# The even mixer's 31-tap convolution: from VectorE to TensorE, in four phases of the tokens and 32-column tiles

## The chip, the cores and the metric

One NeuronCore of one Trainium2 chip runs the whole program. The metric is the device time of one launch in microseconds (us). The engines are TensorE (PE; its weight loads are listed as PEld), VectorE (DVE), ScalarE (ACT), GpSimd (POOL) and SyncE (SP, which only issues DMAs). Each engine runs its own list of instructions in order, and that order is fixed when the program is built. TensorE has two clock levels, 1.2 and 2.4 GHz; the profile's granted clock is the share of the higher one.

## What is computed

A two-layer network for 512 tokens of width 1024 (even mixer, odd mixer), followed by a second two-layer block (a state-space mixer, an attention mixer, and an MLP and a gated embedding in each layer). Only the even mixer is touched:

```python
p = h @ w_in                                  # (512, 5120)
a_val, a_glu, a_gate, b_val, b_gate = split(p)
u = a_val * sigmoid(a_glu)
u = causal_depthwise_conv(u, conv_w, conv_b)  # 31 taps along the tokens, each channel by itself
u = silu(layernorm(u, ln_g, ln_b))            # over the 1024 channels
ya = u * silu(a_gate)
d = multiscale_pool_diff(b_val)               # windows of 2, 4, 8, 16 tokens
yb = (d @ pool_w + pool_b) * pool_scale * silu(b_gate)
return concat(ya, yb) @ w_out
```

All of it is float32.

## The kernel before

Activations lie transposed: a tile is 128 channels (partitions) by 512 tokens. Every large product is made of three TensorE passes (`mm3`, L284 to L286): weight and activation are each split into a high and a low part, and hi·hi, hi·lo and lo·hi are added. An output tile of 128 columns with 1024 inputs takes 24 such matmuls of 512 columns. Its weights (512 KB) come by one DMA from SP into `raw` (two buffers, L264); ACT makes `hi` (three buffers), and `lo = raw - hi` is made by POOL for the first 107 weight tiles and by VectorE after that (`prep`, `on_pool`). The even mixer's own weight tiles are numbers 0 to 57.

In `even` the order is as follows. Four eager output tiles run on the input before the norm; then `xg` (normed input, 8 tiles) is ready. For each of 8 channel tiles `c`, one output tile gives the value and one the gate, and VectorE makes `u` of them. All 31 taps of the convolution are VectorE instructions (`stt`, L240, one tap of one channel tile each) that add into a PSUM bank `cv`; two channel tiles run side by side. This block stands under `later(4000)`, which tells the planner that sets the order to let other work go first. Its last instruction for each channel tile also feeds `csum`, the sum over channel tiles. Then come the pooling branch (`pooled`, four groups), the mean (`mu`, a matmul of `csum` with ones, L554), the subtraction, squares and their sum, eight output tiles for `yb`, eight for the gate `a_gate` (inside which `rms_col` and `spread` of the norm lie, L337 and L366), and last the products `normed`, `gated`, `halved` and eight output tiles for `ya`.

Beside it runs `tables`, which prepares the state-space mixer of a later stage: eight rounds, each with small float32 matmuls (L963, L965, in 32-column tiles), transposes (L971, L989), many small POOL and VectorE operations, and some twenty DMAs from SP. Its matmuls have a very high priority on TensorE, its other work the lowest.

The planner works from its own estimate of times; if an operand comes later on the chip than it thought, the engine's queue waits there.

Of the kernel before, what the change touches and what calls it, by code (L numbers as in the profile page):

```python
# [7 lines left out]
F32 = mybir.dt.float32  # L8
# [3 lines left out]
AF = mybir.ActivationFunctionType  # L12
# [56 lines left out]


def host_layout(i):
    f = {}
# [25 lines left out]
    v.add("g_even", gcols(i["norm_even"][0]))  # L98
    v.add("conv_a_w", np.ascontiguousarray(i["conv_a_w"][0].reshape(KC, 8, 128).transpose(2, 1, 0)).reshape(128, 8 * KC))
    v.add("conv_a_b", cols(i["conv_a_b"][0]))  # L100
    v.add("ln_g", cols(i["ln_a_g"][0]))
# [33 lines left out]
    c.add("chunk", np.repeat(np.arange(64, dtype=np.float32)[None], 128, axis=0))  # L135
    c.add("half", np.repeat(np.repeat(np.eye(2, dtype=np.float32)[::-1], 64, axis=0), 16, axis=1))
    c.add("not0", np.repeat((np.arange(64) > 0).astype(np.float32)[None], 128, axis=0))
    f["consts"] = c.array()
# [18 lines left out]
class Kern:  # L157
# [5 lines left out]
    YA, LNP, SQB, TS = 3, 2, 3, (8, 0, 0)  # L163
    SQX, EPOS = (0, 2, 5), (0, 4)
    BOOST = 400
    on_pool = frozenset(range(107))

# [209 lines left out]
    def consts(self):  # L377
# [6 lines left out]
        self.ident, self.fix, self.eye16, self.chunk, self.not0 = (C(n) for n in ("ident", "fix", "eye16", "chunk", "not0"))  # L384
        self.half = C("half")
        self.halfpi = self.p_const.tile([128, 1], F32, name="halfpi")
# [26 lines left out]
    def even(self, h, behind_norm, extra, tables):  # L413
        nc = self.nc
        hw = self.L("hw", 1, F32, (128, 8 * KC))
        self.ts(hw, self.V("conv_a_w", 0, 8 * KC), 0.5, ALU.mult)

# [50 lines left out]

        us = []
        for c in range(8):  # L470
            th = self.L("th", 2)
            u = self.L("b", 9)
            if c < self.EAGER:
                pv, pg = first[2 * c:2 * c + 2]
                self.mul(th, pg, rs)
                pg = th
                self.mul(u, pv, rs)
                pv = u
            else:
                pv = self.mtile(xg)  # L480
                pg = self.mtile(xg)
            self.act(th, pg, AF.Tanh, scale=0.5)
            self.stt(u, th, 1.0, pv, ALU.add, ALU.mult)
            us.append(u)
            if c == self.EAGER - 1:
                if self.BN == 2:
                    behind_norm()
                extra()
        csum = None
        with self.later(4000):  # L490
            for c in range(0, 8, 2):
                cs = (c, c + 1)
                ps = [self.bank("cv") for _ in cs]
                for j in range(KC - 2, -1, -1):
                    s = KC - 1 - j
                    for q, y in zip(cs, ps):
                        w = hw[:, q * KC + j:q * KC + j + 1]
                        if s == 1:
                            self.act(y[:, 1:], us[q][:, :T - 1], AF.Identity, scale=w, bias=self.V("conv_a_b", q))
                            self.act(y[:, 0:1], self.ones[:, 0:1], AF.Copy, scale=self.V("conv_a_b", q))  # L500
                        else:
                            self.stt(y[:, s:], us[q][:, :T - s], w, y[:, s:], ALU.mult, ALU.add)
                for q, y in zip(cs, ps):
                    self.stt(us[q], us[q], hw[:, q * KC + KC - 1:q * KC + KC], y, ALU.mult, ALU.add)
                    if q == 1:
                        csum = self.L("b", 9)
                        self.add(csum, us[0], us[1])
                    elif q > 1:
                        self.add(csum, csum, us[q])
        conv = us  # L510

# [3 lines left out]
        def pooled(g):  # L515
            w = 2 << g
            ds[g] = []
            for c in range(2):
                pb = self.mtile(xg)
                v = self.L("v", 2)  # L520
                self.act(v, pb, AF.Copy)
                cur, sh = v, 1
                while sh < w:
                    n = self.L("pl", 3)
                    nc.scalar.copy(out=n[:, :sh], in_=cur[:, :sh])
                    self.add(n[:, sh:], cur[:, sh:], cur[:, :T - sh])
                    cur, sh = n, sh * 2
                o = w - 2
                self.mul(cur[:, :w], cur[:, :w], self.fix[:, o:o + w])
                self.stt(v, cur, 1.0 / w, v, ALU.mult, ALU.subtract)  # L530
                ds[g].append(self.split(v, self.LR("d", 6)))

        pooled(0)
        for g in range(4):
# [10 lines left out]
            for c in range(2):  # L545
# [5 lines left out]
                yb.append(self.split(t, self.LR("big", 16), self.V("pool_scale", 2 * g + c)))  # L551

        mu = self.bank("st")
        nc.tensor.matmul(mu, self.ones, csum, start=True, stop=True)  # L554
# [33 lines left out]
        def normed(c):  # L588
            self.mul(conv[c], conv[c], lrs)
            self.act(conv[c], conv[c], AF.Silu, scale=self.V("ln_g", c), bias=self.V("ln_b", c))  # L590

        def gated(c):
            self.mul(conv[c], conv[c], ga[c])

        def halved(c):
            ya.append(self.split(conv[c], self.LR("big", 16)))

# [1142 lines left out]
```

## Time and profile before

| | |
|---|---|
| time, median of 3 runs | 1914.96 us (1912.16 to 1916.82) |
| the profiled execution's own time | 1916.26 us |
| its span, first to last instruction | 1914.5 us |
| mean granted TensorE clock | 0.963 |
| TensorE busy | 1775.2 us (93%) |
| VectorE busy | 1258.0 us (66%) |
| POOL busy | 576.6 us (30%), of it 366 us in the first 500 us |
| DMA | 200.57 MB, mean 105 GB/s |

The even mixer's matmuls on `xg` start at 54 us and its last ones end near 442 us; the odd mixer follows at once. In the page, times are us, the mean of one instruction is in ns, and "idle before" is what the engine stood still ahead of a group, with the one that ended it behind the arrow. A TensorE matmul's duration contains its way through the array; the distance between starts is what it costs in a stream.

### The profile page before, as it was taken

The page shows a single profiled execution, that of the slowest core. Times are in us where ns is not written, and L with a number is a line of the kernel's source. Part 1 is how long each engine was busy: PE and PEld are TensorE (multiplying, and loading weights), DVE is VectorE, ACT ScalarE, POOL GpSimd, SP SyncE. Part 2 cuts the span into 40 slices and gives each one's busy share as a digit, 9 for nine tenths or more (in the row PEclk, how much of TensorE's full clock was granted, in tenths as well). Part 3 has the DMA queues.
Part 4 walks back from the last instruction along what each step waited for, and adds up shares of the span by engine and source line. Part 5 has one row for each costly group of instructions (what it writes and reads, how often), then busy time and mean ns, then how long its engine had stood idle before and what let it go on. Part 6 is the DMA issues. An engine that isn't in the chain of part 4 may idle for free.

```text
span 1914.5 us, 23189 instructions
## 1 busy us (share of the span) xinstructions
PE 1775.2 (93%) x8530; PEld 1426.4 (75%) x8530; DVE 1258.0 (66%) x1916; ACT 764.1 (40%) x1298; POOL 576.6 (30%) x606
## 2 busy tenths in 40 slices
PE   6998889799987797799999999999999999999997
PEld 5776667567766576687888888887778888888886
DVE  8999999976878768745432344478776642244456
ACT  3334332443654553224332242334665432233233
POOL 4889877683667643200000000023000000000002
PEclk7999989899998998899999999999999999999998
DMA  4233233333222378623222223333111222322322
GB/s 150 82 114 98 92 104 116 110 97 100 68 71 78 112 237 280 206 79 104 99 93 94 99 93 95 99 104 110 49 47 52 99 97 90 99 98 90 99 88 94
DMA packets 104290, 200.57 MB, mean 105 GB/s; under 512 B 26737, under 2 KB 57073, under 8 KB 104177
## 3 DMA queue, kind: packets, MB, share of 16 engines
q1 hardware_dynamic: 96496, 182.41, 29.6%
q0 software_dynamic: 2640, 8.65, 1.4%
q10 hardware_dynamic: 5040, 8.04, 1.2%
q8 instruction: 67, 1.10, 0.2%
q14 instruction: 47, 0.38, 0.1%
HBM read 176.38 MB, written 22.02 MB: 104 GB/s over the span
## 4 chain that ended last, share of the span: by engine, by line
PE 62%; DVE 24%; issue 4%; ACT 4%; POOL 3%; DMA 2%; SPq 0%; ACTq 0%; DVEq 0%; POOLq 0%
PE mm L284 18%; PE mm L285 17%; PE mm L286 17%; DVE cv L240 6%; DVE xs L228 2%; POOL lo L228 1%; DVE pl L228 1%; PE pv L1512 1%; DVE e L726 1%; DVE srr L228 1%; DVE xc L240 1%; ACT hi L225 1%; PE sc L285 1%; PE sc L284 1%; PE sc L286 1%
## 5 line engine op out<-in xcount | busy, mean ns | idle before, releaser
L225 ACT ACTIVATE hi<-raw 128x1024 fp32r<-128x1024 f32 (+1 forms) x280 | 292.1, 1045 | 646.9 <-PE mm L285 543.1
L228 DVE TENSOR_TENSOR lo<-raw,hi 128x1024 fp32r<-128x1024 f32 (+1 forms) x185 | 226.8, 1226 | 417.2 <-ACT hi L225 413.7
L286 PE MATMUL mm<-xg,lo 128*128 128x512 f32 x924 | 365.3, 396 | 4.6 <-POOL lo L228 4.6
L284 PE MATMUL mm<-xg,hi 128*128 128x512 f32 x924 | 366.5, 398 | 1.9 <-ACT xs L225 1.4
L285 PE MATMUL mm<-xg,hi 128*128 128x512 f32 x924 | 364.9, 396 | 0.0
L1326 POOL DMA_DIRECT2D pj<-proj x16 | 8.8, 548 | 1036.6 <-DVE t L240 795.8
L228 POOL TENSOR_TENSOR lo<-raw,hi 128x1024 fp32r<-128x1024 f32 (+1 forms) x95 | 234.3, 2469 | 117.5 <-ACT hi L225 106.9
L284 PE MATMUL mm<-hid,hi 128*128 128x512 f32 (+1 forms) x648 | 254.4, 393 | 1.3 <-DVE t L228 1.3
L285 PE MATMUL mm<-hid,hi 128*128 128x512 f32 (+1 forms) x648 | 253.9, 392 | 0.0
L286 PE MATMUL mm<-hid,lo 128*128 128x512 f32 (+1 forms) x648 | 253.7, 392 | 0.0
L286 PEld LDWEIGHTS mm<-xg,lo 128*128 128x128 f32 x924 | 176.6, 191 | 42.7 <-POOL lo L228 5.3
L284 PEld LDWEIGHTS mm<-xg,hi 128*128 128x128 f32 x924 | 176.4, 191 | 41.2 <-ACT xs L225 1.9
L285 PEld LDWEIGHTS mm<-xg,hi 128*128 128x128 f32 x924 | 176.6, 191 | 38.7 <-issue 1.2
L240 DVE SCALAR_TENSOR_TENSOR cv<-b,hw,cv 128x510 f32<-128x510 f32 (+28 forms) x232 | 158.7, 726 | 0.0
L284 PEld LDWEIGHTS mm<-hid,hi 128*128 128x128 f32 x648 | 121.7, 188 | 30.1 <-DVE t L228 1.5
L285 PEld LDWEIGHTS mm<-hid,hi 128*128 128x128 f32 x648 | 121.7, 188 | 28.6
L286 PEld LDWEIGHTS mm<-hid,lo 128*128 128x128 f32 x648 | 121.7, 188 | 28.5
L284 PE MATMUL mm<-y,hi 128*128 128x512 f32 x192 | 78.6, 409 | 5.4 <-ACT y L225 5.4
L286 PE MATMUL mm<-y,lo 128*128 128x512 f32 x192 | 76.7, 400 | 1.3 <-POOL lo L228 1.3
L285 PE MATMUL mm<-y,hi 128*128 128x512 f32 x192 | 76.8, 400 | 0.0
L285 PE MATMUL mm<-big,hi 128*128 128x512 f32 x160 | 68.2, 427 | 8.5 <-DVE big L240 7.6
L284 PE MATMUL mm<-big,hi 128*128 128x512 f32 x160 | 65.3, 427 | 8.5 <-DVE gt L240 5.8
(467 smaller groups left out, 3157.1 us busy)
## 6 DMA issues: line engine op xcount, KB each, us to landing
raw<-in_w_up SPq DMA_DIRECT2D x64, 512.0 KB
raw<-in_w_down SPq DMA_DIRECT2D x64, 512.0 KB
raw<-in_w_in_even SPq DMA_DIRECT2D x40, 512.0 KB
raw<-in_w_in_odd SPq DMA_DIRECT2D x24, 512.0 KB
raw<-in_w_out_even SPq DMA_DIRECT2D x16, 512.0 KB
raw<-in_w_glu SPq DMA_DIRECT2D x16, 512.0 KB
raw<-in_w_gate SPq DMA_DIRECT2D x16, 512.0 KB
raw<-in_w_out_odd SPq DMA_DIRECT2D x16, 384.0 KB
```

Of the source, the lines that this page charges most:

```text
L225: self.nc.scalar.activation(out=out, in_=in_, func=func, scale=scale, bias=bias)
L228: (eng or self.nc.vector).tensor_tensor(out=out, in0=a, in1=b, op=op)
L240: self.nc.vector.scalar_tensor_tensor(out=out, in0=a, scalar=s, in1=b, op0=op0, op1=op1)
L284: mm(out, hi[:, sl], xh, start=start, stop=False)
L285: mm(out, hi[:, sl], xl, start=False, stop=False)
L286: mm(out, lo[:, sl], xh, start=False, stop=stop)
L726: nc.vector.tensor_tensor_scan(out=y, data0=u[:, k], data1=x[:, k], initial=0.0, op0=ALU.mult, op1=ALU.add)
L1326: self.nc.gpsimd.dma_start(out=p, in_=pj[m])
L1512: mm(o, l, r[:, w], start=n == 0, stop=n == 6 * nk - 1)
```

## The change

The convolution leaves VectorE. For each channel tile the gated `u` is written with its tokens sorted into four phases (token mod 4), stored to DRAM (`cu`), and read back sixteen times by SP: for each quarter of 32 channels a tile `z` holds four groups of 8 channels side by side, and on its 128 partitions 8 channels times four phases times four shifts (0 to 3 places). A convolution of 31 taps then is, for each quarter and each group of 8 channels in it, three matmuls that add up (shifts of 0, 4 and 8 columns), in float32, with weights of 128 x 32 in which one column is one channel and one output phase: 48 matmuls a channel tile, each on one of four 32-column tiles of the array (`tile_position=(0, 32*g)`), of 128, 124 and 120 columns. The weights are spread over the block-diagonal form by VectorE (`taps`: three multiplications by a mask for each channel tile). ACT adds the bias and empties PSUM, and the result goes through DRAM again (`cy`, written from ACT's queue, read by SP) to come back as channels by tokens, still in phase order; `gated` puts the tokens back. The matmuls of channel tile c - 2 are traced behind the two output tiles of channel tile c. Apart from that the low parts of weight tiles 0, 2, ..., 56 move from POOL to VectorE.

```diff
-    on_pool = frozenset(range(107))
+    on_pool = frozenset(n for n in range(107) if n > 57 or n % 2)
...
+        def phases(c, u):
+
+            cu = self.dram.tile([128, T], F32, name=f"cu{c}")
+            nc.sync.dma_start(out=cu, in_=u)
+            zs = []
+            for q in range(4):
+                z = self.L("big", 16).rearrange("p (g t) -> p g t", g=4)
+                nc.gpsimd.memset(z[0:96, :, 0:3], 0.0)
+                for a in range(4):
+                    src = bass.AP(cu.tensor, cu.offset + 16384 * q, [[128, 32], [4096, 4], [1, 125 + a]])
+                    nc.sync.dma_start(out=z[32 * a:32 * a + 32, :, 3 - a:128], in_=src)
+                zs.append(z)
+            ready[c] = zs
+
+        def taps(c):
+            wd = self.L("wd", 2, F32, (128, 192))
+            nc.sync.dma_start(out=wd, in_=self.I["conv_a_w"][c])
+            self.act(wd, wd, AF.Copy, scale=0.5)
+            ws = []
+            for k in range(3):
+                w = self.L(*(("sq", self.SQB), ("gt", 3))[c % 2])
+                self.tt(w.rearrange("p (g d o) -> p g d o", g=16, d=8),
+                        wd[:, 64 * k:64 * k + 64].rearrange("p (g o) -> p g o", g=16).unsqueeze(2).to_broadcast([128, 16, 8, 4]),
+                        self.own.unsqueeze(1).unsqueeze(3).to_broadcast([128, 16, 8, 4]), ALU.mult, nc.gpsimd if c in self.TAPP else None)
+                ws.append(w)
+            ready[c] = ready[c], ws
+
+        def convolve(c):
+            zs, ws = ready.pop(c)
+            y = self.bank("cv")
+            for q in range(4):
+                for k in range(3):
+                    for g in range(4):
+                        w = ws[k][:, 32 * (4 * q + g):32 * (4 * q + g) + 32]
+                        with self.after():
+                            nc.tensor.matmul(y[32 * g:32 * g + 32, 128 * q + 4 * k:128 * q + 128], w, zs[q][:, g, 0:128 - 4 * k],
+                                             start=k == 0, stop=k == 2, tile_position=(0, 32 * g))
+            o = self.L("v", 2)
+            for q in range(4):
+                self.act(o[:, 128 * q:128 * q + 128], y[:, 128 * q:128 * q + 128], AF.Identity, bias=self.V("conv_a_b", 4 * c + q))
+            cy = self.dram.tile([T, 128], F32, name=f"cy{c}")
+            nc.scalar.dma_start(out=cy.rearrange("(q p) t -> p q t", p=128), in_=o.rearrange("p (q t) -> p q t", q=4))
+            conv[c] = self.L("b", 9)
+            nc.sync.dma_start(out=conv[c], in_=cy.rearrange("(h p) t -> h (p t)", p=4))
...
+            phases(c, u)
...
-        with self.later(4000):
-            for c in range(0, 8, 2):
...
-                            self.stt(y[:, s:], us[q][:, :T - s], w, y[:, s:], ALU.mult, ALU.add)
...
+            if c:
+                taps(c - 1)
+            if c > 1:
+                convolve(c - 2)
...
+                if g == 0:
+                    if c == 0:
+                        taps(7)
+                    convolve(6 + c)
...
+        csum = self.L("b", 9)
+        for c in range(1, 8):
+            self.add(csum, csum if c > 1 else conv[0], conv[c])
         mu = self.bank("st")
...
         def gated(c):
-            self.mul(conv[c], conv[c], ga[c])
+            v, ga[c] = ga[c], self.L("d", 6)
+            p4 = lambda x: x.rearrange("p (t o) -> p t o", o=4)
+            self.mul(p4(ga[c]), conv[c].rearrange("p (o t) -> p t o", o=4), p4(v))
```

## Rows read from the trace of the kernel before

**Rows 1.** The page: tenths of busy time in 40 slices of 47.9 us, two engines.
```profile
PE   6998889799987797799999999999999999999997
DVE  8999999976878768745432344478776642244456
```
**Rows 2.** Stretches of the even mixer: busy us (instructions) of each engine, clock, DMA.
```profile
54.00:180.00 126.00, 119.31 (x528) 94.01 (x527) 125.93 (x205) 47.38 (x99) 110.41 (x155) 0.97 0.32 102
180.00:250.00 70.00, 58.61 (x244) 45.20 (x243) 70.00 (x85) 25.51 (x60) 63.79 (x80) 0.93 0.34 105
250.00:310.00 60.00, 54.18 (x237) 41.52 (x236) 60.00 (x93) 21.26 (x45) 43.85 (x57) 0.94 0.35 103
...
340.00:390.00 50.00, 35.85 (x150) 26.22 (x150) 47.25 (x97) 25.70 (x61) 34.34 (x43) 0.85 0.40 115
390.00:442.00 52.00, 50.41 (x220) 38.53 (x221) 37.94 (x48) 21.31 (x35) 40.84 (x44) 0.95 0.31 93
```
**Rows 3.** TensorE's waits from 54 to 442 us: us, times, longest.
```profile
PE st L554 <- DVE b L228: 6.4, 1, 6.4
PE mm L284 <- DVE gt L240: 5.8, 1, 5.8
PE mm L286 <- POOL lo L228: 5.3, 3, 2.6
```
**Rows 4.** Groups on TensorE, 54 to 442 us: one of the large products.
```profile
L284 PE MATMUL mm<-xg,hi 128*128 128x512 f32 x288 | 117.3, 410 | 0.0
```
**Rows 5.** TensorE in order of time: start us, us, engine, line, operation.
```profile
434.57 0.40 PE L284 MATMUL mm<-big,hi 128*128 128x512 f32 x1
434.90 0.30 PE L965 MATMUL tab<-tq_wi,cbi 128*32 128x128 f32 x1
434.91 0.30 PE L963 MATMUL tab<-tq_wr,cbr 128*32 128x128 f32 x1
...
435.15 0.38 PE L965 MATMUL tab<-tq_wi,cbi 128*32 128x128 f32 x2
435.46 0.50 PE L285 MATMUL mm<-big,hi 128*128 128x512 f32 x1
435.80 0.40 PE L286 MATMUL mm<-big,lo 128*128 128x512 f32 x1
...
436.03 0.40 PE L284 MATMUL mm<-big,hi 128*128 128x512 f32 x1
```
**Rows 6.** The same view near 733 us: four 32-column tiles one after another.
```profile
732.44 0.68 PE L1100 MATMUL st<-ctile,xc 128*32 128x64 f32 x16 [4.81 <-DVE xc L228]
733.04 0.80 PE L284 MATMUL mm<-y,hi 128*128 128x512 f32 x1
733.64 0.63 PE L285 MATMUL mm<-y,hi 128*128 128x512 f32 x1
734.07 0.63 PE L286 MATMUL mm<-y,lo 128*128 128x512 f32 x1
```
**Rows 7.** Groups on VectorE, 54 to 442 us: the convolution, and a contended subtraction.
```profile
L240 DVE SCALAR_TENSOR_TENSOR cv<-b,hw,cv 128x510 f32<-128x510 f32 (+28 forms) x232 | 158.7, 726 | 0.0
L228 DVE TENSOR_TENSOR d<-v,d 128x512 fp32r<-128x512 f32 x8 | 14.0, 1754 | 0.0
```
**Rows 8.** Low parts of weights: POOL from 54 to 442 us.
```profile
L228 POOL TENSOR_TENSOR lo<-raw,hi 128x1024 fp32r<-128x1024 f32 x54 | 133.4, 2471 | 43.6 <-ACT hi L225 41.9 <-issue 1.6
```
**Rows 9.** Low parts of weights on VectorE, 500 to 1000 us.
```profile
L228 DVE TENSOR_TENSOR lo<-raw,hi 128x1024 fp32r<-128x1024 f32 (+1 forms) x42 | 50.5, 1205 | 91.1 <-ACT hi L225 90.9
```
**Rows 10.** ACT, 54 to 442 us: emptying a 128x128 piece of PSUM.
```profile
L225 ACT ACTIVATE tq_ks<-tab 128x128 f32<-128x128 f32 x8 | 2.1, 268 | 7.7 <-PE tab L965 7.7
```
**Rows 11.** SP's queue: issuing loads of 128 rows of 512 bytes.
```profile
676.39 2.46 SPq L1078 DMA_DIRECT2D gt<-tM  x4
```
**Rows 12.** A stretch in which SP issues such loads without a pause.
```profile
684.00:688.00 4.00, 4.00 (x19) 3.24 (x18) 1.17 (x1) 0.83 (x1) 1.85 (x1) 1.00 0.71 203
```
**Rows 13.** The chain of work, 240 to 395 us: a DMA from issue to landing.
```profile
290.05 2.83 DMA tO<-tq_wr
```
**Rows 14.** TensorE in order of time: the norm's matmuls, and the first on `ya`.
```profile
345.86 2.07 PE L554 MATMUL st<-b,ones 128*128 128x512 f32 x2 [6.43 <-DVE b L228]
378.45 1.90 PE L366 MATMUL st<-ctile,rs_s 128*128 128x128 f32 x8 [4.35 <-DVE rs_s L240]
388.10 1.03 PE L284 MATMUL mm<-big,hi 128*128 128x512 f32 x3 [1.22 <-ACT big L225]
```

More of the change, by code (lines that the diff above doesn't have):

```diff
@@ L68, in pair_n, with conv_rows @@
     return np.ascontiguousarray(r).reshape((128, 32) + a.shape[2:])
+def conv_rows(w):
+    k, a, o, p = np.arange(3)[:, None, None, None], np.arange(4)[:, None, None], np.arange(4)[:, None], np.arange(4)
+    j = KC - 1 - (4 * (4 * k - a + 3) + p - o)
+    taps = np.where(((j >= 0) & (j < KC))[..., None], w[np.clip(j, 0, KC - 1)], np.float32(0))
+    r = taps.reshape(3, 4, 4, 4, 8, 16, 8).transpose(4, 1, 6, 2, 0, 5, 3)
+    return np.ascontiguousarray(r).reshape(8, 128, 192)
 def host_layout(i):
@@ L98, in host_layout @@
     v.add("g_even", gcols(i["norm_even"][0]))
-    v.add("conv_a_w", np.ascontiguousarray(i["conv_a_w"][0].reshape(KC, 8, 128).transpose(2, 1, 0)).reshape(128, 8 * KC))
-    v.add("conv_a_b", cols(i["conv_a_b"][0]))
+    f["conv_a_w"] = conv_rows(i["conv_a_w"][0])
+    v.add("conv_a_b", np.repeat(i["conv_a_b"][0].reshape(32, 32).T, 4, axis=0))
     v.add("ln_g", cols(i["ln_a_g"][0]))
@@ L136, in host_layout @@
     c.add("half", np.repeat(np.repeat(np.eye(2, dtype=np.float32)[::-1], 64, axis=0), 16, axis=1))
+    c.add("own", np.tile(np.repeat(np.eye(8, dtype=np.float32), 4, axis=0), (4, 1)))
     c.add("not0", np.repeat((np.arange(64) > 0).astype(np.float32)[None], 128, axis=0))
@@ L164 @@
     SQX, EPOS = (0, 2, 5), (0, 4)
+    TAPP = ()
     BOOST = 400
-    on_pool = frozenset(range(107))
+    on_pool = frozenset(n for n in range(107) if n > 57 or n % 2)
     def __init__(self, ctx, tc, I, O, vat, cat):
@@ L384, in consts @@
         self.ident, self.fix, self.eye16, self.chunk, self.not0 = (C(n) for n in ("ident", "fix", "eye16", "chunk", "not0"))
-        self.half = C("half")
+        self.half, self.own = C("half"), C("own")
         self.halfpi = self.p_const.tile([128, 1], F32, name="halfpi")
@@ L467, in even @@
             xg.append(self.split(n, self.X()))
-        us = []
+        conv, csum, ready = [None] * 8, None, {}
+        def phases(c, u):
[10 more added lines that the diff above has]
+            ready[c] = zs
@@ L470, in even @@
         for c in range(8):
             th = self.L("th", 2)
-            u = self.L("b", 9)
+            u = self.L("pl", 3)
             if c < self.EAGER:
@@ L476, in even @@
                 pg = th
-                self.mul(u, pv, rs)
-                pv = u
+                m = self.L("v", 2)
+                self.mul(m, pv, rs)
+                pv = m
             else:
@@ L482, in even @@
             self.act(th, pg, AF.Tanh, scale=0.5)
-            self.stt(u, th, 1.0, pv, ALU.add, ALU.mult)
-            us.append(u)
+            p4 = lambda x: x.rearrange("p (t o) -> p t o", o=4)
+            self.stt(u.rearrange("p (o t) -> p t o", o=4), p4(th), 1.0, p4(pv), ALU.add, ALU.mult)
+            phases(c, u)
             if c == self.EAGER - 1:
@@ L488, in even @@
                 extra()
-        csum = None
-        with self.later(4000):
-            for c in range(0, 8, 2):
[L492 to L501, printed above, removed]
-                            self.stt(y[:, s:], us[q][:, :T - s], w, y[:, s:], ALU.mult, ALU.add)
[L503 to L510, printed above, removed]
+            if c:
+                taps(c - 1)
+            if c > 1:
+                convolve(c - 2)
         yb, ds = [], {}
@@ L592, in gated @@
         def gated(c):
[L593 removed]
+            v, ga[c] = ga[c], self.L("d", 6)
+            p4 = lambda x: x.rearrange("p (t o) -> p t o", o=4)
+            self.mul(p4(ga[c]), conv[c].rearrange("p (o t) -> p t o", o=4), p4(v))
         def halved(c):
[L596 removed]
+            ya.append(self.split(ga[c], self.LR("big", 16)))
         for c in range(10 + self.LNP):
```

2 lines of the change are left out of this document (removed).

## The prediction, made before the change was run

> **What bounds the kernel now.** I began with the page's slices: over the first eight, VectorE is at 8 or 9 tenths, and TensorE, elsewhere at 9, drops to 7 and 8 [rows 1]. So I cut the even mixer, 54 to 442 us on TensorE, into stretches. VectorE is busy 126 of 126, 70 of 70 and 60 of 60 us up to 310, TensorE 119, 59 and 54 [rows 2]. A full VectorE need not be the bound: the taps stand last in the planner's order, as filler. The waits of TensorE tell what they delay: 6.4 us for `csum` (b), 5.8 us for a gate tile `gt` that VectorE finished late, 5.3 us for low parts from POOL [rows 3].
>
> What did TensorE lose? Of the large products 1296 lie behind 54 us: 54 tiles of weights, 24 each (288 on each of three lines for `xg` [rows 4]). In a stream they start 0.23 us apart (435.80 to 436.03 [rows 5]): 298 us. The tables' matmuls: from 434.57 plus 0.23 to 435.46, and 0.11 in the wider step to 435.80, is 0.77 us for six records [rows 5], so about 0.13 each; some 195 records, an estimate from 16 groups of 8 and the transposes, make 25. The norm's matmuls add 4 [rows 14]. Together 327 of 388 us: 61 us are lost to waits and to the slower clock behind them. The 1509 instructions in six stretches (the five shown and 130 in the 30 us between them) at 1509/327 = 4.6 per us should have taken 115, 53, 51.5, 28, 33 and 48 us; the losses are 11, 17, 8.5, 2, 17 and 4 us.
>
> The 17 us from 340 to 390 are the norm. `csum` comes at 345.86, the mean's matmul waits 6.43 for it, and 42 us later the first matmul on `ya` starts [rows 14]. TensorE had by then done most of the work that could have covered this chain, and what was left ran at a granted clock of 0.85 [rows 2].
>
> **The change, part by part.** *Taps leave VectorE.* 232 instructions of 158.7 us [rows 7] and 8 more of about 0.73: 164 us out. In: 29 low parts of 1.2 us [rows 9], 35 us; 24 masked weight tiles of 512 elements, a form not in the trace, between 0.73 (a tap) and 1.75 (the contended subtraction [rows 7]), 17 to 42 us, for which I take 22, nearer to the tap. VectorE falls by about 107 of its 371 us here.
>
> So the norm no longer follows the end of the taps. Its chain of 42 us starts when `csum` is done, behind the pooling branch, near 260 us, and has 16 output tiles (16 x 24 x 0.23 = 88 us) ahead of it as cover: the 17 us go. If csum came 46 us later than that, the cover would be gone. The gate wait goes with the queue of taps ahead of it: 8 of the 8.5 us from 250 to 310.
>
> *Low parts leave POOL.* 29 of 2.47 us [rows 8], 72 us. 32 small memsets come in; between nothing and a full low part each, 0 to 79 us, of 12 elements per partition, so I take nothing. Waits for POOL and for the tables' chains make most of the 17 us from 180 to 250 and the 11 before. POOL was busy 64 of 70 there [rows 2], and with a fifth less to do I give back 10 and 4. Ends: 0 and 28.
>
> *The convolution on TensorE.* 384 matmuls of 124 columns on average, each two records. The trace has this form: one takes 0.25 us on its tile (434.90 to 435.15), and another in the next 32 columns starts 0.01 us after it [rows 5]. Four tiles stood in a row once: 16 records of 64 columns in 0.60 us, while large matmuls right after were 0.43 apart, the 1.2 GHz level [rows 6]. There such a record costs what 128 columns cost at full clock, 0.125; one after another 2.0 us. So three or four ran side by side. With four, 12 rounds x 0.25 x 124/128 = 2.9 us, and 0.3 for going in and out (0.77 less four steps of 0.12 [rows 5]): 3.2 us per channel tile, 26 us in all. It adds in full, as TensorE is what counts here. Ends: two side by side, 50 us; none, 98.
>
> The Trainium skill ("TensorEngine Tiling (Array Packing)", Key Properties) says that tiles run independently, but that changing the tiling mode drains TensorE. The 0.3 us agrees. By that rule, a convolution cut apart by large matmuls between its 12 rounds would pay it 96 times, an estimated 29 us instead of 2.4; the edges that tie each matmul behind the last traced one speak against it.
>
> *DMAs and waits.* A channel tile puts 19 DMAs on SP (1 `cu`, 16 `z`, 1 weights, 1 `cy` back) and one on ACT. The nearest rows, 128 rows of 512 bytes, took 0.615 us each to issue [rows 11]: 128 `z` loads are 79 us of SP, in the same queue as the weight loads and the tables' DMAs. While SP issued nothing but such loads and weights, TensorE stayed full (4.00 of 4.00) with the DMA engines at 0.71 [rows 12]. So I take bandwidth as hidden; there is slack of two raw and three high tiles for a late weight load. What is added is a wait ahead of each of 8 convolutions for loads or weights later than planned. Such small waits of TensorE for tables sum to some 15 us over 16 groups, about 1 us each by that estimate, so 0 to 8; convolutions lie two channel tiles behind their inputs, so I take 2.
>
> The skill ("DMA: Bandwidth & Descriptors", Specifications) says that rows under 512 bytes cost a read-modify-write. Twelve of a channel tile's sixteen loads have rows of 500 to 508 bytes; no row shows those. By that rule the 0.71 of rows 12 would near 1, weight loads would come late, and the sum would be that of the first rival below.
>
> *ACT* gets 32 emptyings of 0.27 us [rows 10], 9 us, and 8 small scalings, and loses 16 small ones. It is at most half busy [rows 2]: nothing. If that cover is gone, a PSUM bank of two is held up, not the output tiles' banks. `gated` keeps its count of instructions.
>
> Sum, against the profiled run of 1916.3 (span 1914.5, 1.8 around it): -17 - 8 - 10 - 4 + 26 + 2 = -11, 1905.3. The median of the runs lies 1.3 below the profiled one; I say 1905.
>
> **The rivals.** *SP becomes the bound* (slower). SP works in order: `z` loads wait for `cu` to land, 2.83 us for such a DMA [rows 13], and weight loads queue behind. 79 us plus 8 x 2.8 = 23 us of waits fill 102 of the 126 us to 180 in which the convolutions are due, and weight loads and tables come on top. If nothing is issued in these waits, TensorE stands still for them: 1905 + 23 = 1928. It decides once the queue falls behind TensorE by more than the prefetch, two output tiles (11 us). Also queued there: VectorE's weight tiles wait for TensorE to free buffers, and behind them wait low parts and the pooling branch. For it: the count of issues. Against: rows 12, and that the planner can slide convolutions behind other tiles, with room until the norm.
>
> *Freed time that is not on the path* (no change). The taps were filler, so only the norm and the gate wait come back: -25 + 26 + 2 = +3, 1918 by the median. For it: TensorE was nearly full from 54 to 180 with VectorE at 126 of 126. Against: the POOL waits in rows 3.
>
> *All stalls go*: -61 + 26 = -35, 1880. For it: both elementwise engines then have slack. Against: the tables' chains across engines stay.
>
> *The tiles do not run side by side* as planned: two give +24, 1929; one gives +72, 1977. Against: rows 6.
>
> **How the numbers follow.** Forecast 0.42 (1896 to 1909), all stalls gone 0.15, no change 0.21, SP bound 0.17, array 0.05. A measurement of this kernel tells some 0.3% (6 us) from no change. Faster takes the first two, 0.57; same 0.21; slower 0.22. The range from 1880 to 1928 takes in both outer cases' own values and leaves out the parts beyond them: half of the SP case and most of the array's, about 0.12, and a few hundredths below.
>
> **What would show it.** Right: the mean's matmul without a wait over 1 us, near 260 to 290 us, and the clock near 1.0 through the gate tiles; 3.2 us from the first to the last matmul of a convolution; the even mixer ending on TensorE near 431 us instead of 442. SP as the bound: TensorE waiting for `raw`, `hi` or `z` between 60 and 200 us, and SP's issues without gaps. Freed time off the path: waits for POOL's low parts and for the tables as long as before. Wrong altogether: a convolution of 6 us or more, or TensorE waiting for `cy` at the norm.

## The result, and the profile after

The changed kernel takes 1927.18 us (median of four runs, 1925.44 to 1931.44), the kernel before 1915.03 beside it: 1.0066 of it, with a 95% interval of 1.0055 to 1.0078. That is 12 us slower, where 10 us faster was forecast. The profiled execution took 1925.71 us, its span is 1923.9 (before: 1916.26 and 1914.5). Ratios below are to the kernel before, run on the same chip beside each experiment; differences in us are those of the medians of the two.

The page, its slices of 48.1 us, answers rows 1. VectorE is no longer full from the second slice on, and TensorE is no fuller for it:

```profile
PE   7988898999988797799999999999999999999997
DVE  9633598385887768844532344478776642244456
```

Stretches cut at the same milestones in both kernels: the matmuls on `xg`, then the pooling branch with the gate tiles, then the tiles on `ya`. Columns as in rows 2. First before, then after:

```profile
54.00:257.00 203.00, 184.93 (x805) 144.42 (x804) 202.93 (x299) 77.11 (x165) 179.44 (x240) 0.96 0.32 101
257.00:388.00 131.00, 110.42 (x479) 84.01 (x477) 128.33 (x229) 46.98 (x105) 89.92 (x119) 0.92 0.37 111
388.00:444.00 56.00, 53.44 (x233) 40.49 (x233) 41.56 (x52) 23.78 (x42) 42.84 (x45) 0.94 0.32 98
```

```profile
49.60:297.80 248.20, 216.67 (x1590) 168.39 (x1589) 145.44 (x241) 90.90 (x219) 175.00 (x275) 0.94 0.51 148
297.80:407.40 109.60, 102.42 (x497) 80.24 (x495) 67.73 (x115) 39.03 (x83) 73.61 (x118) 0.97 0.44 132
407.40:456.40 49.00, 46.94 (x198) 37.47 (x199) 33.17 (x37) 20.11 (x29) 11.97 (x5) 0.97 0.30 96
```

The first matmul on `xg` comes 4.5 us earlier. The pooling and gate stretch is 21 us shorter, the one on `ya` 7, and what follows the even mixer 3 us. Everything lost is in one place: the stretch on `xg`, 45 us longer. The view of the convolution's line says where in it:

```profile
L517 PE MATMUL cv<-big,sq x384: 266/272/423, 66.0 to 162.0; 128*32 128x128 f32 x65, 128*32 128x124 f32 x65, 128*32 128x120 f32 x62
L517 PE MATMUL cv<-big,gt x384: 266/269/421, 86.1 to 176.1; 128*32 128x128 f32 x64, 128*32 128x124 f32 x64, 128*32 128x120 f32 x64
```

All eight convolutions run between 66 and 176 us. So the stretch from 54 to 180 us of rows 2, in the kernel after:

```profile
54.00:180.00 126.00, 109.86 (x1125) 86.26 (x1123) 49.95 (x93) 34.92 (x80) 70.44 (x121) 0.92 0.66 189
```

1125 instructions less 768 records of the convolution leave 357, where before there were 528. At the 4.6 per us of the prediction the missing 171 are 37 us of TensorE: 23 to 26 went to the convolution's matmuls (2.9 us each at full clock, below), and 11 to 14 to standing still and to a clock of 0.92 instead of 0.97. VectorE is busy 50 of 126 us where it had been full; DMA went from 0.32 to 0.66.

What TensorE waited for from 45 to 460 us, the answer to rows 3:

```profile
PE tab L1014 <- POOL tq_wr L241: 8.3, 4, 3.7
PE mm L297 <- ACT big L238: 7.1, 2, 4.8
PE mm L299 <- POOL lo L241: 6.2, 2, 4.9
PE cv L517 <- DMA tM<-tq_kq: 4.9, 1, 4.9
PE tab L1016 <- POOL tq_wi L241: 4.6, 2, 4.3
...
PE cv L517 <- DMA big<-cu: 1.1, 3, 0.7
```

The waits for `csum` and for the gate tile are gone, as forecast. Waits for POOL took their place; for `z` itself (`big<-cu`) TensorE stands only 1.1 us. All lines of this view from 45 to 460 us add up to 41 us, and to 43 in the kernel before, so in sum TensorE waits as long as it did. Which of these is a cause, and which only the last link, the chain of work tells better. Its shares by line from 60 to 180 us, before and then after:

```profile
by line: DVE cv L240 54.8%; DVE pl L228 6.8%; DVE b L240 5.3%; DVE sv_xs_p L240 5.0%; issue 2.6%; DVE xg L228 2.4%; PE mm L286 2.3%; PE mm L285 2.1%; PE mm L284 2.1%; DVE sv_sp L240 2.0%; DVE v L240 1.9%; DVE b L228 1.9%; DVE sv_sq L243 1.3
```

```profile
by line: DMA raw<-in_w_in_even 15.4%; SPq L492 10.5%; PE mm L297 8.3%; PE cv L517 7.8%; PE mm L298 7.6%; PE mm L299 7.4%; DMA tO<-tq_wr 6.3%; DMA wd<-in_conv_a_w 5.0%; POOL lo L241 3.9%; issue 3.5%; POOL tq_wr L241 3.2%; DMA tR<-tq_rt 2.8%;
```

Before, the taps on VectorE were the chain. After, it runs through SP issuing `z` (L492) and through transfers that stand behind it: weights, the convolution's weights `wd`, the tables' stores. One lap of it in order of time (start us, us, what):

```profile
100.15 0.63 SPq L1033
100.82 4.96 DMA tO<-tq_wr
...
105.94 0.79 POOL tq_wr L241
106.81 1.06 POOL tq_wr L241
107.92 0.41 PE tab L1014 x2
...
113.86 1.07 ACT hi L238
114.95 1.14 DVE lo L241
116.08 5.99 DMA wd<-in_conv_a_w
122.13 4.02 DMA raw<-in_w_in_even
```

This store of 64 KB takes 4.96 us to land, where rows 13 had 2.83, and the load of 96 KB 5.99; two other such stores in the same chain took 2.90 and 2.56. SP's queue shows why they also start late (start us, us, queue, line, transfer and count):

```profile
95.78 1.80 SPq L492 DMA_DIRECT2D big<-cu  x4
97.67 0.38 SPq L277 DMA_DIRECT2D raw<-in_w_in_even  x1
...
105.55 8.98 SPq L492 DMA_DIRECT2D big<-cu  x16
114.63 0.38 SPq L485 DMA_DIRECT2D cu<-pl  x1
115.06 0.43 SPq L525 DMA_DIRECT2D b<-cy  x1
115.58 0.40 SPq L277 DMA_DIRECT2D raw<-in_w_in_even  x1
116.08 0.38 SPq L498 DMA_DIRECT2D wd<-in_conv_a_w  x1
117.22 4.71 SPq L492 DMA_DIRECT2D big<-cu  x7
```

Nothing gets past sixteen issues that take 8.98 us. From 62 to 180 us SP spends 98 of 118 us on issues, and its longest pause is 3.0 us. Two engines stand behind that, each in order. ACT waits for `wd`, with a weight tile's high part queued behind it, and POOL for the tables' stores to give up a buffer:

```profile
ACT wd L238 <- DMA wd<-in_conv_a_w: 19.1, 3, 6.8
```

```profile
POOL tq_wr L241 <- DMA tO<-tq_wr: 36.5, 4, 15.7
```

For the second product tile (`tq_wi`) it is another 8.8 us. The kernel before has no `wd`, and its POOL waited 2.9 us in all for stores to `tO`.

### The profile page after: what moved, and what is told of

The parts are those of the page before. It is cut to its first block, busy times and chain, and to the rows that moved or that the text cites. A ratio compares the mean times of both kernels' runs of the same rounds, so it can differ in the third digit from the quotient of the medians.

```text
span 1923.9 us, 24932 instructions
## 1 busy us (share of the span) xinstructions
PE 1790.6 (93%) x9298; PEld 1440.5 (75%) x9298; DVE 1125.4 (58%) x1728; ACT 768.3 (40%) x1322; POOL 519.7 (27%) x609
## 4 chain that ended last, share of the span: by engine, by line
PE 64%; DVE 12%; POOL 7%; DMA 6%; issue 5%; ACT 5%; SPq 2%; ACTq 0%; POOLq 0%; DVEq 0%
PE mm L297 19%; PE mm L298 18%; PE mm L299 18%; POOL lo L241 2%; DVE lo L241 1%; ACT hi L238 1%; DMA raw<-in_w_in_even 1%; PE pv L1563 1%; DVE xs L241 1%; DMA raw<-in_w_in_odd 1%; DVE xc L253 1%; POOL tq_wr L241 1%; PE sc L298 1%; PE sc L297 1%; PE sc L299 1%
## 5 line engine op out<-in xcount | busy, mean ns | idle before, releaser
L241 DVE TENSOR_TENSOR lo<-raw,hi 128x1024 fp32r<-128x1024 f32 x214 | 265.7, 1242 | 476.1 <-ACT hi L238 456.0
L241 POOL TENSOR_TENSOR lo<-raw,hi 128x1024 fp32r<-128x1024 f32 (+1 forms) x66 | 161.5, 2449 | 127.1 <-ACT hi L238 116.0
L299 PE MATMUL mm<-big,lo 128*128 128x512 f32 x160 | 65.1, 410 | 2.4 <-DVE lo L241 2.4
```

The lines of the kernel that those rows point to most:

```text
L241: (eng or self.nc.vector).tensor_tensor(out=out, in0=a, in1=b, op=op)
L299: mm(out, lo[:, sl], xh, start=False, stop=stop)
```

## The experiments

**What is the relief worth, without any convolution in its place?** The taps out of the kernel before, and then the low parts moved as well. (Both leave out 29 of 31 taps.)

```diff
-                for j in range(KC - 2, -1, -1):
+                for j in range(KC - 2, KC - 3, -1):
```

> The kernel before with 29 of the 31 taps left out (two taps of the convolution remain); everything else as before. It shows what VectorE's 158 us of taps cost there. The prediction's step (17 us of the norm, 8 of the gate, 14 of POOL and tables come back once VectorE is free) says 1874 to 1880. If the waits are of another cause and only the norm comes back: 1892 to 1900. If nothing comes back: 1911 to 1919.

> The kernel before with 29 of 31 taps left out and the low parts of weight tiles 0, 2, ..., 56 on VectorE: both engines relieved as in the change, with no price on TensorE or SP. It is what the change could give back at most. With the taps out alone 1903 (before 1917 beside it). The prediction gave POOL's relief 14 us: 1886 to 1892. If its waits are the tables' chains: 1895 to 1903. The changed kernel less the convolution's 26 us of TensorE would be 1901.

Measured: 0.9918 [0.9898, 0.9938] for the taps, 14 us faster; 0.9842 [0.981, 0.9875] for both, 29 us. The first is less than the prediction's step and comes nearest to the range in which only the norm comes back; the second fits the range with POOL's 14 us on top. The low parts alone, in the kernel before and taken back in the changed one:

```diff
-    on_pool = frozenset(range(107))
+    on_pool = frozenset(n for n in range(107) if n > 57 or n % 2)
```

> The kernel before with only the low parts of weight tiles 0, 2, ..., 56 moved from POOL to VectorE; the taps stay on VectorE. VectorE is full until 340 us there, so 35 us more delay csum and the norm: 1920 to 1940 under both theories, unless POOL's low parts were what TensorE waited for, then 1905 to 1912.

> The changed kernel with all low parts of the even mixer's weights back on POOL; the convolution stays on TensorE. Two theories for the 12 us lost. Theory S (SP's queue): the convolution's 128 loads hold SP from 62 to 178 us, the tables' stores queue behind them, so the tables pile up on POOL from 180 to 310 us; then 72 us more of low parts on POOL must make it worse: 1933 to 1945. Theory T (TensorE): the convolution's 26 us stand in full on the bounding engine and the old waits are planner's errors that stay whoever makes the low parts: 1923 to 1931, as the changed kernel (1927).

Measured: moved in the kernel before, 1.0043 [1.0031, 1.0055], a loss of 10 us; taken back in the changed kernel, 1.0148 [1.0129, 1.0167], 30 us over the kernel before instead of 12. So this half of the change pays only where VectorE has been emptied first. Where TensorE got the 29 us back is seen in the pooling and gate stretch. It is 131 us long before, 119 with the taps out (first line) and 104 with both (last line), where its clock is 1.00 instead of 0.92. TensorE's waits in it add up to 19.5, 13.5 and 3.3 us: with the taps alone out the waits for VectorE's `csum` and gate tile are gone, but waits for the tables and others stand in their place.

```profile
253.00:371.70 118.70, 105.08 (x477) 79.98 (x475) 69.91 (x124) 41.60 (x91) 90.18 (x118) 0.96 0.43 123
...
47.70:259.40 211.70, 189.34 (x831) 146.04 (x830) 154.45 (x262) 92.94 (x216) 178.10 (x266) 0.96 0.36 107
259.40:363.40 104.00, 100.68 (x493) 79.47 (x492) 55.62 (x82) 34.48 (x66) 67.33 (x103) 1.00 0.46 132
```

The stretch on `xg`, where the low parts were to give 14 us, didn't get shorter: 211.7 us against 203, with 26 more of TensorE's instructions in it, nearly all of them the tables', and POOL as busy as before (178 us of 212; 179 of 203). The time that the low parts left on POOL was taken by the tables, which moved up. From 29 us below the kernel before to 12 above it: the convolution on TensorE costs 41 us. TensorE's waits from 45 to 460 us tell the same: 43 us before, 28 with both reliefs and no convolution, 41 with it. So 13 of the 41 us are waits that the convolution brought, beside 23 to 26 us of matmuls.

**How much of the 41 is its matmuls?** Two thirds of them out, then all. (The first computes one of three sums, the second none.)

```diff
-                for k in range(3):
+                for k in range(1):
```

> The changed kernel with two of the three matmuls of each sum left out (shifts of 4 and 8 columns): 128 instead of 384, all transfers, weights and waits kept. TensorE's price for the convolution falls by two thirds of 26 us. Theory T (TensorE's own work is in the path): 1909 to 1914 on the scale where before is 1915 and changed 1927. Theory S (the loads for the convolution and SP's queue set the pace from 62 to 178 us): the freed time turns into longer waits for z, 1919 to 1927.

```diff
-            y = self.bank("cv")
...
-                            nc.tensor.matmul(y[32 * g:32 * g + 32, 128 * q + 4 * k:128 * q + 128], w, zs[q][:, g, 0:128 - 4 * k],
...
-                self.act(o[:, 128 * q:128 * q + 128], y[:, 128 * q:128 * q + 128], AF.Identity, bias=self.V("conv_a_b", 4 * c + q))
+                self.act(o[:, 128 * q:128 * q + 128], zs[q][:, 0], AF.Identity, bias=self.V("conv_a_b", 4 * c + q))
```

> The changed kernel without the convolution's 384 matmuls; everything else of it stays: phases, stores, sixteen loads and weight tiles for each channel tile, the four emptyings on ACT (which now read one group of each tile z instead of PSUM), the way back through DRAM. The convolution's values are therefore not computed. Without the whole convolution the kernel stood at 0.9842 (1887 us), with all of it at 1.0066 (1927 us): 40 us between them. Theory A, the transfers and small operations cost by themselves what is over the 26 us of matmuls, whoever runs on TensorE: 1901 us, 0.991 to 0.995. Theory B, they cost only where TensorE stands still in order for a convolution whose tiles z are not there yet, or for what is queued behind one: 0.984 to 0.988, near the kernel without the convolution. Rival C, the loads hold up weights and tables by more than that: over 0.997.

Measured: 1.0017 [1.0002, 1.0031] and 1.0038 [1.0022, 1.0055]. Taking 17 us of matmuls away gave back 9, taking all 26 only 4. The first lies at the edge of what was expected if the loads set the pace, the second in the third rival's range, in which the loads hold up weights and tables. The second has to be read with care, because the edit made a wait of its own: ACT now meets `z` before TensorE does, and stands for it.

```profile
ACT v L238 <- DMA big<-cu: 47.2, 25, 5.4
```

So it doesn't price the transfers. What both runs suggest is that the matmuls don't simply add: the chain of the run with a third of them, from 60 to 180 us, is the loads and little else.

```profile
by line: DMA raw<-in_w_in_even 16.7%; SPq L492 15.3%; DMA big<-cu 13.9%; DMA cu<-pl 12.0%; issue 5.7%; PE mm L299 3.2%; DVE sv_sp L253 2.9%; DVE pl L253 2.9%; PE mm L297 2.4%; PE mm L298 2.4%; DVE xg L241 2.3%; POOL lo L241 2.0%; POOL tq_u 
```

**SP's queue.** The sixteen loads issued by ACT; one load in place of four, four times as wide (a tile of 2048 columns, cut up for the other users of its buffers); then one load in all, of a quarter of the bytes, which all sixteen groups read (the convolution is not computed, every matmul is kept).

```diff
-                    nc.sync.dma_start(out=z[32 * a:32 * a + 32, :, 3 - a:128], in_=src)
+                    nc.scalar.dma_start(out=z[32 * a:32 * a + 32, :, 3 - a:128], in_=src)
```

> The changed kernel with the sixteen z loads of each channel tile issued from ACT's queue instead of SP's. ACT then carries some 60 to 80 us of issues more, of 406 us in which it is busy about 150. Theory S: the tables run beside the convolution again, POOL is less full from 180 to 310 us, 1905 to 1918. Theory T: 1923 to 1931. If ACT's own order is hurt by the waits for cu, over 1931, and the trace shows ACT waiting at these issues.

```diff
-                z = self.L("big", 16).rearrange("p (g t) -> p g t", g=4)
...
+            z = self.Q4().rearrange("p (g t) -> p g t", g=16)
+            nc.gpsimd.memset(z[0:96, :, 0:3], 0.0)
+            for a in range(4):
+                src = bass.AP(cu.tensor, cu.offset, [[128, 32], [4096, 16], [1, 125 + a]])
+                nc.sync.dma_start(out=z[32 * a:32 * a + 32, :, 3 - a:128], in_=src)
```

> The changed kernel, whole computation, with z as one tile of 2048 columns: four loads a channel tile instead of sixteen (512 rows of some 500 bytes each), one memset instead of four; the same bytes and rows. Of SP's 128 z issues 32 remain, each perhaps longer. Theory S: the tables' stores no longer queue on SP, TensorE's waits for POOL between 60 and 310 us shrink, 1908 to 1918. Theory T, or if the issue costs go by rows and not by DMAs: 1924 to 1930.

```diff
-            for a in range(4):
-                src = bass.AP(cu.tensor, cu.offset, [[128, 32], [4096, 16], [1, 125 + a]])
-                nc.sync.dma_start(out=z[32 * a:32 * a + 32, :, 3 - a:128], in_=src)
+            nc.sync.dma_start(out=z[:, 0:4, :], in_=cu.rearrange("p (g t) -> p g t", g=4))
```

> The kernel with four loads a channel tile (1.0022 of the kernel before), with one load of a quarter of the bytes in place of the four, and all sixteen groups of matmuls read that quarter: the convolution computes on the wrong data, with every matmul kept. If issues or bytes of the loads still cost, 0.999 or less (6 us and more back). If the four loads were already cheap enough and what is left lies elsewhere: 1.0008 to 1.0037, as it was.

Measured: 1.0025 [1.0012, 1.0038], 1.0022 [1.0008, 1.0037] and 1.0027 [1.0016, 1.0039]. The first two give back 6 and 8 us, less than expected if the queue were all of it. That the queue held the tables up shows on POOL: from 54 to 180 us it is busy 70 us in the changed kernel, and 106 with the loads on ACT or with four (110 before). The third gives no more, though the DMA engines' share in that stretch falls from 0.85 (four loads; sixteen had 0.66) to 0.54. So after four loads there is no sign that their number or bytes still cost time. What is late then is POOL's tables again: TensorE's first wait with four loads, 8.3 us in the changed kernel, is

```profile
PE tab L1024 <- POOL tq_wr L253: 15.3, 6, 3.9
```

**The tables' chains.** First their buffers and stores: a third buffer, the stores on ACT's queue, a third buffer on top of the best kernel so far, and the same third buffer in the kernel before as a control.

```diff
-                wr, wi = F("wr", 2), F("wi", 2)
+                wr, wi = F("wr", 3), F("wi", 3)
```

> The changed kernel with a third buffer for each of the tables' two product tiles (wr, wi). In the changed kernel POOL waits 36.5 us for stores of these tiles (tO) to land, in the kernel before hardly at all, and TensorE waits 19 us for POOL behind it. If these stores, held up on SP and on the DMA engines by the convolution's loads, are what made the new waits: 1915 to 1921 on the scale of before 1915, changed 1927, and POOL's wait for tO falls below 15 us. If the waits of TensorE are of another origin: 1925 to 1929.

```diff
-                        nc.sync.dma_start(out=tO[64 * k:64 * k + 64, 512 * q:512 * q + 512].rearrange("n (a g m) -> n g a m", a=2, g=2)[:, g2],
+                        nc.scalar.dma_start(out=tO[64 * k:64 * k + 64, 512 * q:512 * q + 512].rearrange("n (a g m) -> n g a m", a=2, g=2)[:, g2],
```

> The changed kernel with the tables' 64 tO stores issued from ACT's queue instead of SP's. If the place in SP's queue behind the convolution's loads is what makes them late: 1914 to 1921. If the DMA engines themselves are late, or ACT pays with its own time for 64 issues of 0.6 us: 1924 to 1930.

> Whole computation: four z loads a channel tile, the first 18 low parts on VectorE, and three buffers for the tables' product tiles. Without the buffers it stood at 0.999 of before. If the stores of the tables are the rest of the new waits: 1904 to 1911 (before 1915). If not, 1912 to 1918.

> The kernel before with the third buffer for wr and wi, nothing else. Control: POOL hardly waits for these stores there, so the buffers alone should be worth nothing: 1912 to 1918. If it is faster by 4 us or more, the gain of the other kernels with three buffers is no sign of the convolution's transfers.

Measured: 1.0058 [1.004, 1.0075], 1.0072 [1.0049, 1.0095], 1.0026 [1.001, 1.0042]; control 1.006 [1.0044, 1.0076]. The first two came out as expected if these stores were not the cause, the other two outside every range. The control matters most: a buffer that by itself can only remove a wait cost the kernel before 13 us. Its program is planned anew around it (POOL's order differs from 86.8 us on, where one of the tables' products now stands ahead of a low part), and its stretch on `ya` takes 63 us instead of 56. A single run that moves the time by less than that, with the plan redone, isn't proof of the cause that it was made for; this holds for the 6 and 8 us above too, though there two different edits agree and the chain of work names the same queue.

Next the tables left out of both kernels (the odd mixer then computes on zeros), and last half of POOL's part of the first four groups moved to VectorE:

```diff
-        cr, ci, pr, pi, m8, th8 = small
...
+            for t, w in ((tS, 1024), (tO, 1024), (tM, 256), (tR, 512)):
+                nc.sync.dma_start(out=t.rearrange("p (k n) -> p k n", n=128), in_=z.unsqueeze(1).to_broadcast([128, w // 128, 128]))
```

> The changed kernel with the odd mixer's tables left out: their arithmetic on POOL, VectorE and ACT, their matmuls and transposes on TensorE and all their transfers but four stores of zeros per group, so the odd mixer computes on zeros. It stands beside the kernel before with the same left out. The changed kernel is 12 us longer than the one before with the tables in (1.0066). Theory, the new waits are those of TensorE for the tables' chains, whose stores and POOL steps are delayed by the convolution's transfers and memsets: without tables the difference goes to between -6 and +2 us, since the measured relief of 30 us then stands against 26 us of matmuls with nothing behind. Rival, the waits are the convolution's own (its loads, its order between the output tiles): the difference stays between +8 and +14 us. Rival, the planner's order only: anything, with TensorE's idle in the stretch on xg as large as before.

> The kernel before with the odd mixer's tables left out in the same way, as the measure for the changed kernel without them. About 200 records on TensorE of 0.13 us go, 26 us, and the waits for the tables' chains: some 1875 us. All theories expect the same of this one; what tells them apart is the difference between the two.

Measured: 0.9782 [0.9762, 0.9802] with the change and 0.9706 [0.9685, 0.9727] without it. The difference stays, at 14 us. Leaving the tables out is worth 54 us in the kernel before and 52 in the changed one, so the change made them no dearer in sum: the theory that their chains alone are what it lost falls. But the pair doesn't set 41 us of convolution against 29 of relief either. Without tables the kernel before has no norm stall to be relieved of: in its pooling and gate stretch TensorE is busy 92 of 95 us, and the wait for `csum` is not there. And with the tables out of the way another wait shows itself in the changed kernel, TensorE standing for `z`, where it was 1.1 us with the tables:

```profile
PE cv L517 <- DMA big<-cu: 12.9, 6, 5.0
```

```profile
by line: PE mm L297 17.8%; PE mm L298 16.3%; PE mm L299 16.2%; SPq L492 14.9%; PE cv L517 12.6%; DMA big<-cu 10.7%; DMA cu<-pl 5.7%; issue 2.3%; SPq L277 1.7%; DVE lo L241 1.0%; ACT hi L238 0.9%; SPq L525 0.4%; SPq L485 0.0%
```

**A version that beats both.** The relief taken further, step by step, with nothing left out: the first 18 low parts all on VectorE, on top of four loads; then half of the first tables on VectorE, alone and on top of both.

```diff
-    on_pool = frozenset(n for n in range(107) if n > 57 or n % 2)
+    on_pool = frozenset(n for n in range(107) if n > 57 or n > 17 and n % 2)
```

> As the kernel with four z loads, and besides the low parts of all of the first 18 weight tiles on VectorE (of the later ones every second, as changed): VectorE is some three quarters idle between 80 and 180 us in the changed kernel. If POOL is late there, 3 to 8 us below the kernel with four loads; if not, within 3 us of it.

```diff
-    SHARED, OWN, HOT, TLATE = 4, 8, 9000, 8000
+    SHARED, OWN, HOT, TLATE = 0, 8, 9000, 8000
```

> The changed kernel with one constant changed: the second half of the tables' work (the products that end in tO, and the angles) of the first four groups goes from POOL to VectorE, which has room since the taps left it. Nothing is left out. Theory, tables' chains on a full POOL hold TensorE up: 1.002 to 1.004 of the kernel before, where the changed kernel has 1.0066. Rival, POOL and the tables only wait for something else: 1.0055 to 1.0078 as it was.

> The same move on top of four loads a channel tile and the first 18 low parts on VectorE, which together stood at 0.9993 of the kernel before. Nothing is left out. Theory, the tables' chains hold TensorE up: 0.994 to 0.997, faster than both kernels. Rival, no more is to be had there: 0.998 to 1.001.

Measured: 0.9993 [0.9977, 1.0009]; 1.0032 [1.0021, 1.0044]; and all together 0.9945 [0.9924, 0.9966]: 1908.18 us, 8 us faster than the kernel before beside it, where the changed kernel is 12 slower. The two steps with the tables came out as the theory of their chains on a full POOL had it, and the low parts gave 4 us, as expected if POOL was late. Each of these steps is smaller than the 13 us of the control, though; only the 20 us that all of them give is larger. Its stretches:

```profile
45.60:291.10 245.50, 221.71 (x1642) 175.63 (x1641) 205.56 (x430) 102.00 (x258) 129.55 (x205) 0.94 0.65 168
291.10:386.30 95.20, 94.75 (x452) 76.55 (x450) 33.08 (x55) 29.73 (x47) 39.78 (x47) 1.00 0.38 116
```

VectorE is used again (206 of 246 us on `xg`), POOL falls from 175 to 130 us, and the pooling and gate stretch runs almost without a gap at full clock. TensorE's waits from 45 to 460 us are down to 28 us again.

## Why the prediction was wrong, point by point

**Right in kind, 11 us short: the norm and the gate.** Both waits left TensorE's list, and the mean's matmul runs near 224 us, even earlier than foretold. But with the taps alone out only 14 us came back where 17 + 8 were forecast: the tables' waits stood behind those two in the same stretch. The rest of that stretch came with the low parts; in the changed kernel, which has both reliefs, it lost 21 us. Its clock is 1.00 from 355 to 408 us, as was to be seen if the step held:

```profile
355.00:408.00 53.00, 50.72 (x257) 40.33 (x256) 28.08 (x45) 21.27 (x41) 33.50 (x54) 1.00 0.41 123
```

**Right: the price of the matmuls; wrong: that they run in one piece.** One whole convolution in TensorE's order of time, with its neighbours:

```profile
159.15 0.39 PE L299 MATMUL mm<-xg,lo 128*128 128x512 f32 x1
159.47 2.75 PE L517 MATMUL cv<-big,sq 128*32 128x128 f32 x96
162.15 0.50 PE L297 MATMUL mm<-xg,hi 128*128 128x512 f32 x1
162.49 0.40 PE L298 MATMUL mm<-xg,hi 128*128 128x512 f32 x1
```

From 159.15 to 162.49 are 3.34 us, less 0.46 for the two large products: 2.9 us, forecast 3.2. Four of the eight run like this, in 2.7 to 3.2 us from the first to the last matmul. The other four are spread over 8.7 to 11.6 us, beyond the 6 us that the prediction named as a sign of being wrong: in them TensorE runs large products, or stands, in order, for a table's tile from POOL or for a transfer. Two of these waits:

```profile
133.37 0.42 PE L1016 MATMUL tab<-tq_wi,cbi 128*32 128x128 f32 x1 [4.26 <-POOL tq_wi L241]
...
175.07 1.47 PE L517 MATMUL cv<-big,gt 128*32 128x128 f32 x24 [4.88 <-DMA tM<-tq_kq]
```

In the whole one, four tiles run side by side, and going in and out costs 0.1 us on either side. The Trainium skill ("TensorEngine Tiling (Array Packing)", Key Properties) says that tiles run independently but that a change of mode drains TensorE. Both agree with these rows. Its second half costs little here, 0.2 us a time, and the 96 changes behind the estimate of 29 us did not arise: the trace has the 768 records in 22 runs.

**Right in size: the weight tiles on VectorE.** 22 us were taken for 24, and they took 18: these are 18 of the tiles, and the six made before 45 us took 3.9 us.

```profile
L241 DVE TENSOR_TENSOR sq<-wd,ctile 128x512 f32<-128x512 f32 x9 | 8.1, 949 | 9.3 <-PE cv L517 4.9 <-ACT wd L238 4.3
L241 DVE TENSOR_TENSOR gt<-wd,ctile 128x512 f32<-128x512 f32 x9 | 6.2, 747 | 7.5 <-PE cv L517 7.5
```

The memsets on POOL, taken at nothing, are that: 104 ns each.

**Right in size, wrong in place: the low parts, 14 us.** The prediction gave back "10 and 4" of TensorE's waits on `xg` because POOL would have a fifth less to do. In that stretch nothing came back even without a convolution. POOL was not a fixed load with waits behind it: the tables filled what was freed. What the low parts are worth comes later, where the tables are then done, and only once the taps are out: 15 us of the 29 that both gave. That the 15 lie beside the 14 is partly luck. The relief was 29 us where 39 stood in the sum: 10 us short, 11 at the norm and gate less 1 here. The rival of freed time off the path had this sign right: in the changed kernel TensorE's waits for POOL's low parts are 6.2 us (before 5.3) and for its table tiles 12.9 (before 5.1).

**Wrong: the DMAs and waits, "I take 2".** The convolution costs 41 us where 26 + 2 were forecast: 13 us over. In place of 2 us, TensorE's waits grew by 13 (28 without the convolution, 41 with it), and few of them are waits of the convolution's own matmuls for `z`. The count of SP's issues was right (0.615 us each taken, 8.98 us for sixteen measured, 0.56). The failing sentence is the one that followed from rows 12, that bandwidth and issues are hidden because TensorE stayed full for 4 us while SP issued loads. Four microseconds are less than the prefetch that was then in hand, and say nothing of a queue that is nearly full for 118. What stood in that queue besides, `wd` with ACT waiting for it, and the tables' stores with POOL waiting, the prediction counted as issues but not as waits: ACT was put down at "nothing" by its busy time, while what hit it was 19.1 us of standing still with weights queued behind.

The rival that SP becomes the bound said 1928 and named these signs: issues without gaps, and a convolution or weights late between 60 and 200 us. The chain of work bears it out, and SP's few pauses. It was only part of it, though: relieving SP gives back 6 to 8 us and uncovers POOL's tables behind it. That its 1928 lies beside the 1927 measured is luck: it has no loss of relief in it, and 10 of the 23 us are that. In the version that beats both, the loads gave 8 us, the low parts 4 more, half of the tables' work 6 by itself, and all together 20, near their sum of 18: that one of the two limits hides the other's relief is not shown. The 10 and the 13 us make the 23 between the sum of -11 and the +12 measured.

**Short rows.** Twelve of sixteen loads have rows of 500 to 508 bytes. "DMA: Bandwidth & Descriptors" (Specifications) of the Trainium skill has rows under 512 bytes pay a read-modify-write; by that the DMA engines' share would near 1. It was 0.66 from 54 to 180 us, at 189 GB/s, which is the same share for each GB/s as in rows 12 (0.71 at 203). With four loads it was 0.85 at 207, so there each byte took more of the engines. But one load, whose rows are 2 KB (its page has 1024 more packets of that size, 128 for each channel tile), was no faster than four loads of which three have short rows (1.0027 and 1.0022), so no cost of short rows shows in the time. A long DMA of each kind was not timed by itself.

**Open.** How the 13 us over the forecast divide between SP's queue, the landing of transfers at twice the DMA share, and the planner's new order. The control with a third buffer shows that a new order can be worth as much by itself. Nor do TensorE's summed waits follow the time closely in the runs between: 36 us at 1.0022, 39 at 1.0027. Loading all `wd` ahead, so that ACT never waits for them, was not tried.

## What to carry to other kernels

Price relief and load by stretch, and for an engine whose work can slide ask what will fill the room that is made: here the tables took POOL's, so the waits stayed. For a queue that works in order, write down everything else that stands in it and who waits for that, on ACT and POOL too; an engine's busy time says nothing of the small load it will wait for. Two reliefs are not a sum: here the tables' waits stood behind the norm's. Undo a change that has two halves by halves: one half (low parts to VectorE) cost 10 us alone and saved 15 beside the other.

## What the runs showed of the hardware

An issue of these loads on SP costs by the transfer, not by its bytes: the 128 loads of some 64 KB (128 rows each) took 70 us, 0.55 each, and the 32 loads of some 256 KB (512 rows each), in the kernel with four, 17.4 us, 0.54 each. The first four of these:

```profile
63.31 1.92 SPq L502 DMA_DIRECT2D big<-cu  x4
```

Under that load a small transfer can land late, but need not: in the changed kernel's chain stores of 64 KB took 2.56, 2.90 and 4.96 us and a load of 96 KB 5.99, at a mean DMA share of 0.66, against 2.83 for 64 KB before [rows 13] at 0.35 [rows 2]. And float32 matmuls on four 32-column tiles really overlap: 48 of them, 124 columns on average, in 2.75 us, where one alone holds its tile for 0.25 us [rows 5].
